# One packed weight input for a decoder trunk: every weight slab is stored as 8 KB rows, and the conv state arrives by channel

## The chip, the cores and the metric

The kernel runs on 1 core of one Trainium2 chip. The metric is the device time of one execution in microseconds. Before the change it is 1344.36 us (median of 3 runs, 1343.42 to 1346.48). The profiled execution of the same kernel took 1343.75 us, of which 1342.0 us lie between its first and last instruction (the span).

## What is computed

One layer of a decoder trunk, for 512 prompt tokens and 32 sample tokens (8 sequences of 4) with d_model 1024. All arithmetic is fp32; each big product is made of three fp32r products (a high part and a low part of each operand).

```
def layer(x, c, conv_prev, attend, w):
    mod = silu(c) @ w['w_ada'] + w['b_ada']             # 6 x 1024 columns: shifts, scales, gates
    h = rmsnorm(x, norm1) * (1 + sc1) + sh1
    bg, cg, xin, q, kc, vc, ks, vs, kw, vw, nsa_g, merge_g = split_columns(h @ w['w_in'])
    v, conv_new = short_conv(cg * xin, conv_prev, w['w_conv'], w['b_conv'])   # width 3, per channel
    y_a = (bg * v) @ w['w_out_conv']
    o_b = attend(q, gates, kv_cmp, kv_sel, kv_win)      # compressed, selected and window branches
    y_b = o_b @ w['w_o_nsa']
    x = x + g1 * ((ga * y_a + gb * y_b) @ w['w_out'])
    h2 = rmsnorm(x, norm2) * (1 + sc2) + sh2
    x = x + g2 * ((silu(h2 @ w['w_gate']) * (h2 @ w['w_up'])) @ w['w_down'])
```

The compressed branch multiplies blocks of cached K/V rows by `w_phi1` (2 x 2048 x 128). `conv_prev` is `state_conv`, the last 2 conv inputs of each of the 8 sample sequences: 16 rows of 1024 channels.

## The kernel before, in words

Activations lie transposed in SBUF: 128 channels on the partitions, 8 chunks of channels (KC), 544 tokens along the free side, worked in two halves of 288 and 256 tokens. A weight is read as a *slab* of 8 row blocks x 256 columns, 1 MB (`slab`, lines 164 to 168), into one of three `raw` buffers, by one DMA of the SP queue whose rows are 256 columns = 1 KB (512 B for `w_phi1` and for part of `w_down`). `split` (lines 170 to 178) makes a high part `wh` on ACT (line 176) and a low part `wl` on DVE (line 177) of 128 columns; each has two buffers. `mm3` (lines 180 to 183) issues the three matmuls on PE. Eight chunks x three matmuls x two halves make one linear of 48 matmuls.

Stages in order: loading and transposing x, and the compression of the cached rows with the first 8 `w_ada` slabs between (lines 357 to 574); the K, V and q projections (580 to 709); the short conv, interleaved with the attention of the sample sequences (712 to 967); the conv's output projection (983); the prompt attention with the other `w_ada` slabs and the gate `gb` between (1001 to 1180); the output projections, and the FFN.

Two loaders have loops of their own. `phi_load` (395) reads half of `w_phi1`, 16 row blocks of 128 columns. The q slabs (683 to 689) take two DMAs each, and the `w_o_nsa` slabs (1199 to 1206) four.

GpSimd (POOL) gathers the paged cache rows by indirect DMA: `gt`, 128 rows of 8 KB, 16 times (line 428, two buffers, copied by DVE at 438 and transposed by PE at 446 into `xt`), and `sraw`, 128 rows of 16 KB, 8 times (line 789, transposed by PE at 850 into `kt`).

At the start of the conv stage the SP queue loads the table `tb` (719) and the conv state `st`, 16 partitions of 4 KB (727 to 728). PE transposes `st` in 8 small transposes into the PSUM tile `stp` (732), and DVE copies it to `stT` (733), 128 channels x 8 x 16. Only a POOL copy per conv chunk reads `stT` (745). After the transposes in program order come a generator `fill` (943 to 951), whose steps are half linears of the conv (`cg`, `xin`, `bg` for each chunk), and `sample_gen` (793), which starts with the small products `sx` of q and the keys (805, 807), takes softmaxes of them with `tb` on DVE and ACT (811 to 819, result `px`), lets three more steps of `fill` run, and multiplies `px` on PE (822). `lin`, `stp`, `imp` and `kt` share one PSUM tag of five buffers.

The order of the instructions on each engine is not the program's. A planner orders them by the program's order, by which inputs its own cost model holds ready, and by free buffers. Each engine and each DMA queue then works its own list strictly in order. So the loads of `new_win_sample` (1326), which stand in the FFN's code, are issued from 25 us on.

Of the kernel before, what the change touches and what calls it, by code (L numbers as in the profile page):

```python
# [9 lines left out]
F32 = mybir.dt.float32  # L10
# [8 lines left out]
D = 1024  # L19
KC = 8  # L20
# [13 lines left out]
FC = FF // 128  # L34
# [5 lines left out]
C_KV = 4096  # L40
C_GATE = 5632
# [58 lines left out]
def build(tc, a, o):  # L100
# [19 lines left out]
    def tp_ps(nm):  # L120
        return ps.tile([128, 512], F32, tag="g", bufs=5, name=nm)
# [37 lines left out]
    def raw_tile(n):  # L159
        return wpool.tile([128, 2048], F32, tag="raw", bufs=3, name=nm(n))  # L160

    last_slab = [None]

    def slab(src, c0, nk=8, ncol=256, k0=0):
        t = raw_tile("raw")
        v = t[:, 0:nk * ncol].rearrange("p (k f) -> p k f", k=nk)
        last_slab[0] = sync.dma_start(v, src[k0 * 128:(k0 + nk) * 128, c0:c0 + ncol].rearrange("(k p) f -> p k f", p=128))
        return v

    def split(view, nk=8, perm=None):  # L170
        wh = wpool.tile([128, 8, 128], F32R, tag="wh", bufs=2, name=nm("wh"))
# [46 lines left out]

    cT = cst.tile([128, 8, 32], F32, name="cT")
    pool.memset(cT, 0.0)  # L220
    w_ada, b_off = a["w_ada"], 0

    def mod_slab(s):
        v = slab(w_ada, s * 256)
        p = tp_ps(nm("modp"))
        for k in range(KC):
            for hh in range(2):
                j = (k % 2) * 2 + hh
                pe.matmul(p[32 * j:32 * j + 32, 0:128], lhsT=cT[:, k, :], rhs=v[:, k, hh * 128:(hh + 1) * 128], start=(k < 2), stop=(k >= 6))  # L229
# [163 lines left out]
    rws = []  # L393

    def phi_load(v):
        rw = raw_tile("rphi").rearrange("p (k f) -> p k f", k=16)
        sync.dma_start(rw, a["w_phi1"][v].rearrange("(k p) f -> p k f", p=128))
        rws.append(rw)

    def phi_split(v, qt):  # L400
        qv = lambda t: t.rearrange("p (s c) f -> p s c f", s=2)[:, :, 2 * qt:2 * qt + 2, :]
# [178 lines left out]
    def kv_type(ty, rp, x32=None):  # L580
        sps = acc_ps(nm("sps"))
        for v in range(2):
            sl = slab(a["w_in"], C_KV + ty * 512 + v * 256)
            stage = rp.tile([128, 4, 256], F32, tag="stage", bufs=2, name=nm("stage"))
            for gp in range(2):
                dst = rp.tile([128, NT], F32, tag="kvT", bufs=2, name=nm("kvT"))
                linear(split(sl[:, :, gp * 128:(gp + 1) * 128]), h, lambda hf, p: act.activation(dst[:, hcols(hf)], p, AF.Copy))
                while kvp:
                    kvp.pop(0)()
                kvp.append(lambda v=v, gp=gp, dst=dst, stage=stage: kv_post(ty, v, gp, dst, stage, sps, rp, x32))  # L590
# [79 lines left out]
        cmp_prompt(v, x32, rp)  # L670
    kv_type(2, rp)

    sl = slab(a["w_in"], C_GATE, ncol=128)
    linear(split(sl), h, lambda hf, p: act.activation(gT[0:48, hcols(hf)], p[0:48, :], AF.Sigmoid))
    while kvp:
        kvp.pop(0)()
# [5 lines left out]
    pool.memset(qbd, 0.0)  # L682
    for gp in range(2):
        for rp_ in range(2):
            t = raw_tile("rq")
            tv = t.rearrange("p (k g f) -> p k g f", k=8, g=2)
            for gg in range(2):
                c0 = C_Q + (2 * gp + gg) * 256 + rp_ * 128
                sync.dma_start(tv[:, :, gg, :], a["w_in"][:, c0:c0 + 128].rearrange("(k p) f -> p k f", p=128))
            for r2 in range(2):  # L690
                r = rp_ * 2 + r2
                ch = gp * 4 + r
                w = split(tv[:, :, :, r2 * 64:(r2 + 1) * 64], perm=lambda z: z.rearrange("p k (g f) -> p k g f", g=2))
# [12 lines left out]
                for n in range(2):  # L706
                    sync.dma_start(q_dr[gp][n][:, r * TP:(r + 1) * TP], hl[n].bitcast(F32))
# [16 lines left out]
        off += w_  # L724
    t_sel, t_win, t_cmp, t_new, t_idx, t_rs, t_gs, t_gb = tbs

    st = cv.tile([16, D], F32, name="st")
    sync.dma_start(st, a["state_conv"])
    stT = cv.tile([128, 8, 16], F32, name="stT")
    p = tp_ps("stp")  # L730
    for k in range(KC):
        pe.transpose(p[:, k * 16:(k + 1) * 16], st[:, k * 128:(k + 1) * 128], ident[0:16, 0:16])
    dve.tensor_copy(stT, p[:, 0:128].rearrange("p (k n) -> p k n", k=8))
    ncv = cv.tile([128, 8, 18], F32, name="ncv")

    conv_w = {}
# [33 lines left out]

    def slab_for(nme, k):
        if k % 2 == 0:
            conv_w[nme] = slab(a["w_in"], {"cg": C_CG, "xin": C_XIN, "bg": C_BG}[nme] + k * 128)
        return conv_w[nme]

    csv = a["cache_sel"].rearrange("n t w -> (n t w)").rearrange("(x y) -> x y", y=8 * 512)
# [156 lines left out]

    def ga_linear(k):
        if k % 2 == 0:
            gsl[k // 2] = slab(a["w_in"], C_MERGE + k * 128)
        ga = gas[k] = gap_.tile([128, NT], F32, tag="ga", bufs=3, name=nm("ga"))
        w = split(gsl[k // 2][:, :, (k % 2) * 128:(k % 2) * 128 + 128])
        if k < GAF:
            return linear_gen(w, h, lambda hf, p: evac(ga[:, hcols(hf)], p))  # L940
        linear(w, h, lambda hf, p: act.activation(ga[:, hcols(hf)], p, AF.Sigmoid))
# [39 lines left out]
    C = yinf  # L981

    def y_a(k2):
        sy = slab(a["w_out_conv"], k2 * 256)
        for kk in range(2):
            k = k2 * 2 + kk
            cs = slice(kk * 128, kk * 128 + 128)
            if k >= GAF:
                ga_linear(k)
            else:  # L990
                act.activation(gas[k], gas[k], AF.Sigmoid)
            ga = gas[k]
            linear(split(sy[:, :, cs]), (yh, yl), lambda hf, p: dve.tensor_mul(C[:, k, hcols(hf)], p, ga[:, hcols(hf)]))
# [41 lines left out]
        pool.tensor_copy(vm[rs, :, r, :], vcp[rs].rearrange("p (g d) -> p g d", g=4))  # L1035
    def gb_gen():
        for k2 in range(4):
            sg = slab(a["w_in"], C_MERGE + 1024 + k2 * 256)
            for kk in range(2):
                k = k2 * 2 + kk  # L1040
                wh, wl = split(sg[:, :, kk * 128:(kk + 1) * 128])
# [155 lines left out]
    for k in range(KC):  # L1197
        to_hilo(oT[:, k, :], oh[:, k, TS:NT], ol[:, k, TS:NT])
    for k2 in range(4):
        t = raw_tile("wo")  # L1200
        for gp in range(2):
            for gg in range(2):
                pr = slice(gg * 64, gg * 64 + 64)
                r0 = (2 * gp + gg) * 256
                sync.dma_start(t[pr, gp * 1024:(gp + 1) * 1024].rearrange("p (r f) -> p r f", r=4), a["w_o_nsa"][r0:r0 + 256, k2 * 256:(k2 + 1) * 256].rearrange("(r d) f -> d r f", d=64))
        sy = t.rearrange("p (k f) -> p k f", k=8)
        for kk in range(2):
            k = k2 * 2 + kk
            cs = slice(kk * 128, kk * 128 + 128)
# [42 lines left out]
        yield  # L1252

    for k2 in range(4):
        so = slab(a["w_out"], k2 * 256)
        for kk in range(2):
            v = so[:, :, kk * 128:(kk + 1) * 128]
            if k2 == 0:
# [72 lines left out]
    for c in range(FCA, FC):  # L1331
        ffn_tiles(f6b, c)
    for c2 in range(1, FC // 2):
        sg, su = slab(a["w_gate"], c2 * 256), slab(a["w_up"], c2 * 256)
        if c2 <= DEC_B:
            win_shift(c2 - 1)
        for cc in range(2):
# [46 lines left out]
    posts = []  # L1384
    for m in range(KC):
        if m % 2 == 0:
            sc_ = slab(a["w_down"], m * 128, nk=6, ncol=256, k0=16)
        ra = slab(a["w_down"], m * 128, nk=16, ncol=128, k0=0)
        vs = [(ra[:, 0:8, :], 0, 8), (ra[:, 8:16, :], 8, 8), (sc_[:, :, (m % 2) * 128:(m % 2) * 128 + 128], 16, 6)]
        pls = [lin_ps(nm("dn"))[:, 0:HW[q]] for q in range(2)]  # L1390

# [19 lines left out]
_SHAPES = {  # L1411
    "x_prompt": (512, 1024), "x_sample": (32, 1024), "c_prompt": (1, 1024), "c_sample": (8, 1024),
    "cache_cmp": (80, 128, 512), "cache_sel": (80, 128, 512), "cache_win": (8, 512, 512),
    "state_conv": (16, 1024), "page_table": (8, 8), "w_ada": (1024, 6144), "b_ada": (6144,), "norm1": (1024,),
    "w_in": (1024, 7728), "w_conv": (3, 1024), "b_conv": (1024,), "w_out_conv": (1024, 1024),
    "pe_cmp": (2, 32, 64), "w_phi1": (2, 2048, 128), "w_phi2": (2, 128, 64), "w_o_nsa": (1024, 1024),
    "w_out": (1024, 1024), "norm2": (1024,), "w_gate": (1024, 2816), "w_up": (1024, 2816),
    "w_down": (2816, 1024), "norm_f": (1024,),
}
_OUTS = [  # L1420
    ("y_prompt", (512, 1024), (1, 512, 1024)), ("y_sample", (32, 1024), (8, 4, 1024)),
# [25 lines left out]
```

## Time and profile before

| | |
|---|---|
| median of 3 runs | 1344.36 us |
| profiled execution | 1343.75 us |
| its span, first to last instruction | 1342.0 us |
| PE busy | 1310.5 us, 98% of the span |
| DVE, ACT, POOL busy | 49%, 40%, 5% |
| SP's DMA queue | 149.98 MB in 133302 packets |
| POOL's DMA queue (gathers, window loads) | 41.95 MB in 4608 packets |

PE, DVE, ACT and POOL are TensorE, VectorE, ScalarE and GpSimd; SP issues most DMAs. In timelines a row gives the start in us, the duration, the engine, the line, the instruction, what it writes and reads, its shape and how many were merged; a bracket gives the idle time of that engine before it and what ended it. A duration of a matmul covers its pipeline, so neighbours overlap; the distance of two starts is what one costs.

### The profile page before, as it was taken

The page shows a single profiled execution, that of the slowest core. Times are in us where ns is not written, and L with a number is a line of the kernel's source. Part 1 is how long each engine was busy: PE and PEld are TensorE (multiplying, and loading weights), DVE is VectorE, ACT ScalarE, POOL GpSimd, SP SyncE. Part 2 cuts the span into 40 slices and gives each one's busy share as a digit, 9 for nine tenths or more (in the row PEclk, how much of TensorE's full clock was granted, in tenths as well). Part 3 has the DMA queues.
Part 4 walks back from the last instruction along what each step waited for, and adds up shares of the span by engine and source line. Part 5 has one row for each costly group of instructions (what it writes and reads, how often), then busy time and mean ns, then how long its engine had stood idle before and what let it go on. Part 6 is the DMA issues. An engine that isn't in the chain of part 4 may idle for free.

```text
span 1342.0 us, 25662 instructions
## 1 busy us (share of the span) xinstructions
PE 1310.5 (98%) x10840; PEld 1210.6 (90%) x10840; DVE 654.3 (49%) x1570; ACT 537.5 (40%) x1065; POOL 70.3 (5%) x123
## 2 busy tenths in 40 slices
PE   7999999997999999999999999999999999999997
PEld 6788899996999999899777777999999999999996
DVE  5559332343454454426687676667433333333335
ACT  6335233432332334324776776435323223222223
POOL 2101030001011110001000000000000000000000
PEclk8999999998999999999999999999999999999999
DMA  9996036872535562754457336532223223133221
GB/s 330 313 331 231 33 112 188 275 218 83 215 130 196 185 213 95 195 132 131 124 152 199 101 110 176 155 126 64 64 64 95 95 65 124 56 87 87 87 64 67
DMA packets 138025, 193.56 MB, mean 144 GB/s; under 512 B 4818, under 2 KB 124762, under 8 KB 132919
## 3 DMA queue, kind: packets, MB, share of 16 engines
q1 hardware_dynamic: 133302, 149.98, 36.5%
q0 software_dynamic: 4608, 41.95, 8.3%
q8 instruction: 85, 1.39, 0.5%
q14 instruction: 30, 0.24, 0.1%
HBM read 174.47 MB, written 25.76 MB: 149 GB/s over the span
## 4 chain that ended last, share of the span: by engine, by line
PE 95%; DMA 2%; DVE 1%; ACT 1%; issue 0%; SPq 0%; ACTq 0%; DVEq 0%
PE lin L181 19%; PE lin L182 19%; PE lin L183 19%; PE dn L181 3%; PE dn L182 3%; PE dn L183 3%; PE acc L1133 3%; PE ptp L1139 3%; PE phi L462 2%; PE phi L460 2%; PE phi L461 2%; PE xt L446 2%; PE modp L229 2%; PE kt L850 2%; PE sp L1108 1%; PE sp L1109 1%
## 5 line engine op out<-in xcount | busy, mean ns | idle before, releaser
L181 PE MATMUL lin<-h_hi,wh 128*128 128x288 f32 (+1 forms) x1648 | 479.4, 291 | 0.0
L182 PE MATMUL lin<-h_lo,wh 128*128 128x288 f32 (+1 forms) x1648 | 475.2, 289 | 0.0
L183 PE MATMUL lin<-h_hi,wl 128*128 128x288 f32 (+1 forms) x1648 | 473.8, 288 | 0.0
L181 PEld LDWEIGHTS lin<-h_hi,wh 128*128 128x128 f32 x1648 | 311.1, 189 | 9.4 <-issue 8.1
L182 PEld LDWEIGHTS lin<-h_lo,wh 128*128 128x128 f32 x1648 | 310.7, 189 | 0.5
L183 PEld LDWEIGHTS lin<-h_hi,wl 128*128 128x128 f32 x1648 | 310.1, 188 | 0.3
L177 DVE TENSOR_TENSOR wl<-raw,wh 128x1024 fp32r<-128x1024 f32 x132 | 159.9, 1212 | 244.5 <-ACT wh L176 244.2
L176 ACT ACTIVATE wh<-raw 128x1024 fp32r<-128x1024 f32 x132 | 137.9, 1045 | 300.0 <-PE lin L182 211.4
L181 PE MATMUL dn<-f_hi,wh 128*128 128x256 f32 (+1 forms) x352 | 101.9, 290 | 0.0
L182 PE MATMUL dn<-f_lo,wh 128*128 128x256 f32 (+1 forms) x352 | 101.3, 288 | 0.0
L183 PE MATMUL dn<-f_hi,wl 128*128 128x256 f32 (+1 forms) x352 | 101.0, 287 | 0.0
L1115 ACT ACTIVATE P<-P,nms 128x512 f32<-128x512 f32 (+3 forms) x128 | 70.6, 555 | 18.8 <-DVE nms L1114 17.9
L1114 DVE CUSTOM_DVE_ANT_0 P<-sp,ta 128x512 f32<-128x512 f32 (+3 forms) x128 | 57.5, 482 | 31.0 <-PE sp L1102 23.5
L183 PEld LDWEIGHTS dn<-f_hi,wl 128*128 128x128 f32 x352 | 66.3, 188 | 0.0
L181 PEld LDWEIGHTS dn<-f_hi,wh 128*128 128x128 f32 x352 | 66.2, 188 | 0.0
L182 PEld LDWEIGHTS dn<-f_lo,wh 128*128 128x128 f32 x352 | 66.2, 188 | 0.0
L460 PE MATMUL phi<-xh,wph 128*128 128x512 f32 x128 | 54.0, 422 | 0.0
L461 PE MATMUL phi<-xh,wpl 128*128 128x512 f32 x128 | 52.1, 407 | 0.0
L462 PE MATMUL phi<-xl,wph 128*128 128x512 f32 x128 | 52.0, 408 | 0.0
L448 ACT ACTIVATE xh<-xt 128x512 fp32r<-128x512 f32 x64 | 34.8, 597 | 32.3 <-PE xt L446 31.4
L449 DVE TENSOR_TENSOR xl<-xt,xh 128x512 fp32r<-128x512 f32 x64 | 41.0, 684 | 13.1 <-ACT xh L448 13.1
L1139 PEld LDWEIGHTS ptp<-ident,P 128*128 128x128 f32 x320 | 35.7, 141 | 10.9 <-issue 8.9
(370 smaller groups left out, 2110.2 us busy)
## 6 DMA issues: line engine op xcount, KB each, us to landing
raw<-in_w_in SPq DMA_DIRECT2D x26, 1024.0 KB, 6.6
raw<-in_w_ada SPq DMA_DIRECT2D x24, 1024.0 KB, 9.3
raw<-in_w_gate SPq DMA_DIRECT2D x11, 1024.0 KB, 5.4
raw<-in_w_up SPq DMA_DIRECT2D x11, 1024.0 KB, 5.4
wraw<-in_cache_win POOLq DMA_DIRECT2D x8, 1024.0 KB, 7.0
raw<-in_w_down SPq DMA_DIRECT2D x8, 1024.0 KB, 5.7
out_new_win_sample<-in_cache_win SPq DMA_DIRECT2D x8, 1016.0 KB, 10.5
rq<-in_w_in SPq DMA_DIRECT2D x8, 512.0 KB, 12.0
```

What stands on the lines that cost most here:

```text
L176: act.activation(oh, view, AF.Copy)
L177: dve.tensor_sub(ol, view, oh.bitcast(F32))
L181: pe.matmul(p, lhsT=wh[:, k, :], rhs=xh, start=start, stop=False)
L182: pe.matmul(p, lhsT=wh[:, k, :], rhs=xl, start=False, stop=False)
L183: pe.matmul(p, lhsT=wl[:, k, :], rhs=xh, start=False, stop=stop)
L449: dve.tensor_sub(xlb[v][:, lp * 512:lp * 512 + 512], p, xo.bitcast(F32))
L460: pe.matmul(po, lhsT=w_h, rhs=mh, start=first, stop=False)
L461: pe.matmul(po, lhsT=w_l, rhs=mh, start=False, stop=False)
L462: pe.matmul(po, lhsT=w_h, rhs=ml, start=False, stop=last)
L1114: dve.tensor_tensor_reduce(out=t[:, 0:n], in0=sps[br], in1=t_dist[:, 512 - n:512], scale=-hs, scalar=3e38, op0=ALU.add, op1=ALU.min, accum ...
L1115: act.activation(t[:, 0:n], t[:, 0:n], AF.Exp, scale=-1.0, bias=nms[:, c:c + 1], accum_out=sums[:, c:c + 1])
L1139: pe.transpose(tp[:, r * 128:(r + 1) * 128], P[br, r][:, 128 * j:128 * j + 128], ident)
```

## The change

The weights come as one input `wt` of 128-partition slabs, laid out before the launch. Each slab is one DMA of 128 contiguous rows, 8 KB for a full slab (6 KB for the tails of `w_down`, 4 KB for the gate slab). The two DMAs of a q slab, and the four of a `w_o_nsa` slab, become one each. `phi_load` goes through `slab`. The conv state comes as 128 channels x 128 numbers and is loaded straight into `stT`; the tile `st`, the eight transposes and the copy are gone. Nothing else in the program's order is changed.

```
+def _slabs():
+    r = np.arange(1024).reshape(8, 128)
+    ...
+    for v in range(2):
+        d["phi", v] = ("w_phi1", np.arange(2048).reshape(16, 128) + 2048 * v, np.arange(128))
+    for s in range(24):
+        add(("ada", s), "w_ada", r, s * 256, 256)
+    ...
-    def slab(src, c0, nk=8, ncol=256, k0=0):
-        t = raw_tile("raw")
-        v = t[:, 0:nk * ncol].rearrange("p (k f) -> p k f", k=nk)
-        last_slab[0] = sync.dma_start(v, src[k0 * 128:(k0 + nk) * 128, c0:c0 + ncol].rearrange("(k p) f -> p k f", p=128))
-        return v
+    def slab(*key):
+        nk, ncol = len(SLABS[key][1]), len(SLABS[key][2])
+        v = raw_tile("raw")[:, 0:nk * ncol]
+        last_slab[0] = sync.dma_start(v, a["wt"][SLAB_AT[key], :, 0:nk * ncol])
+        return v.rearrange("p (k f) -> p k f", k=nk)
...
     def phi_load(v):
-        rw = raw_tile("rphi").rearrange("p (k f) -> p k f", k=16)
-        sync.dma_start(rw, a["w_phi1"][v].rearrange("(k p) f -> p k f", p=128))
-        rws.append(rw)
+        rws.append(slab("phi", v))
...
-            t = raw_tile("rq")
-            tv = t.rearrange("p (k g f) -> p k g f", k=8, g=2)
-            for gg in range(2):
-                c0 = C_Q + (2 * gp + gg) * 256 + rp_ * 128
-                sync.dma_start(tv[:, :, gg, :], a["w_in"][:, c0:c0 + 128].rearrange("(k p) f -> p k f", p=128))
+            tv = slab("q", gp, rp_).rearrange("p k (g f) -> p k g f", g=2)
...
-    st = cv.tile([16, D], F32, name="st")
-    sync.dma_start(st, a["state_conv"])
     stT = cv.tile([128, 8, 16], F32, name="stT")
-    p = tp_ps("stp")
-    for k in range(KC):
-        pe.transpose(p[:, k * 16:(k + 1) * 16], st[:, k * 128:(k + 1) * 128], ident[0:16, 0:16])
-    dve.tensor_copy(stT, p[:, 0:128].rearrange("p (k n) -> p k n", k=8))
+    sync.dma_start(stT.rearrange("p k n -> p (k n)"), a["state_conv"])
...
-        t = raw_tile("wo")
-        for gp in range(2):
-            for gg in range(2):
-                ...
-                sync.dma_start(t[pr, gp * 1024:(gp + 1) * 1024]...)
-        sy = t.rearrange("p (k f) -> p k f", k=8)
+        sy = slab("o", k2)
...
+    st = np.asarray(inputs["state_conv"]).reshape(16, 8, 128)
+    arrs["state_conv"] = np.ascontiguousarray(st.transpose(2, 1, 0)).reshape(128, 128)
```

The other calls of `slab` name their slab by a key in place of a source and a column, and load the same numbers into the same places.

## Rows read from the trace of the kernel before

**Rows 1.** The page: the busy time of the engines, and the shares of the chain that ended last.

```profile
PE 1310.5 (98%) x10840; PEld 1210.6 (90%) x10840; DVE 654.3 (49%) x1570; ACT 537.5 (40%) x1065; POOL 70.3 (5%) x123
PE 95%; DMA 2%; DVE 1%; ACT 1%; issue 0%; SPq 0%; ACTq 0%; DVEq 0%
```

**Rows 2.** The waits of PE over the whole run, the longest first: the tile it stood before, what ended the wait, us in total, times, the longest.

```profile
PE stp L732 <- DMA st<-in_state_conv: 8.7, 1, 8.7
PE xtp L507 <- DMA xr<-in_x_prompt: 5.7, 1, 5.7
PE xt L446 <- DVE gt L438: 1.8, 1, 1.8
PE yt L1365 <- DVE x L1360: 1.5, 1, 1.5
...
PE kt L850 <- DMA sraw<-in_cache_sel,ixs: 0.5, 1, 0.5
```

**Rows 3.** The timeline of PE around the transposes of the conv state.

```profile
304.71 0.32 PE L805 MATMUL sx<-kcs,qbd 128*32 128x63 f32 x8
304.84 0.29 PE L807 MATMUL sx<-kn,qbd 128*32 128x64 f32 x8
313.83 1.03 PE L732 MATMUL stp<-ident,st 16*128 16x16 f32 x8 [8.70 <-DMA st<-in_state_conv]
314.80 0.61 PE L181 MATMUL lin<-h_hi,wh 128*128 128x288 f32 x1
...
318.08 0.37 PE L182 MATMUL lin<-h_lo,wh 128*128 128x288 f32 x1
318.30 0.29 PE L183 MATMUL lin<-h_hi,wl 128*128 128x288 f32 x1
318.43 0.29 PE L181 MATMUL lin<-h_hi,wh 128*128 128x288 f32 x1
...
327.03 0.33 PE L822 MATMUL imp<-px,tb 128*128 128x64 f32 x2
```

**Rows 4.** Stretches of the start and of this place: us, busy time (and instructions) of PE, PEld, DVE, ACT and POOL, the granted clock of PE as a share of 2.4 GHz, the busy share of the 16 DMA engines, GB/s.

```profile
14.70:16.50 1.80, 0.01 (x1) 0.02 (x1) 0.83 (x2) 1.72 (x3) 0.00 (x0) 1.00 1.07 402
18.00:20.00 2.00, 2.00 (x15) 1.67 (x13) 1.84 (x4) 1.98 (x5) 0.18 (x1) 0.50 1.04 299
24.00:26.00 2.00, 2.00 (x33) 1.43 (x35) 0.53 (x1) 1.98 (x3) 0.75 (x1) 0.83 1.08 319
305.00:308.00 3.00, 0.14 (x12) 0.00 (x0) 1.71 (x2) 2.40 (x3) 0.00 (x0) 1.00 0.29 107
308.00:313.80 5.80, 0.00 (x0) 0.00 (x0) 0.36 (x4) 0.00 (x0) 0.00 (x0) 0.50 0.71 234
313.80:318.00 4.20, 4.17 (x21) 4.13 (x22) 0.98 (x10) 0.44 (x2) 0.20 (x1) 0.50 0.00 0
318.00:320.00 2.00, 2.00 (x17) 2.00 (x16) 0.00 (x0) 0.18 (x1) 0.00 (x0) 0.94 0.00 0
```

**Rows 5.** The same place on the other engines: SP's queue, then ACT, then DVE (three timelines). `wh` and `wl` at 298.72 to 301.04 and at 304.70 to 307.02 are the weights of the first `cg` and the first `xin` linear.

```profile
307.56 0.32 SPq L707 DMA_DIRECT2D q_dr1l<-ql  x1
307.98 0.37 SPq L719 DMA_DIRECT2D tb<-in_tab_b  x1
308.44 0.39 SPq L728 DMA_DIRECT2D st<-in_state_conv  x1
...
298.72 1.06 ACT L176 ACTIVATE wh<-raw 128x1024 fp32r<-128x1024 f32 x1 [2.21 <-PE lin L182]
304.70 1.06 ACT L176 ACTIVATE wh<-raw 128x1024 fp32r<-128x1024 f32 x1 [2.21 <-PE lin L182]
314.15 0.19 ACT L816 ACTIVATION_READ_ACCUMULATOR px<-sxs,n 128x1 f32 x1
319.82 0.41 ACT L741 ACTIVATE cg<-lin 128x288 f32<-128x288 f32 x1 [5.48 <-PE lin L183]
...
313.44 0.28 DVE L801 TENSOR_TENSOR gm<-tb,gT 48x128 f32<-48x128 f32 x1 [5.91 <-DMA tb<-in_tab_b]
314.90 0.29 DVE L733 COPY stT<-stp 128x128 f32<-128x128 f32 x1 [0.74 <-PE stp L732]
315.30 0.25 DVE L819 TENSOR_SCALAR px<-px,rc 128x63 f32<-128x63 f32 x1
323.67 1.23 DVE L177 TENSOR_TENSOR wl<-raw,wh 128x1024 fp32r<-128x1024 f32 x1 [8.11 <-ACT wh L176]
327.71 0.16 DVE L825 COPY G<-imp 128x3 f32<-128x3 f32 x1 [1.36 <-PE imp L823]
```

**Rows 6.** The chain that ended last, its first pieces: start, us, what.

```profile
5.47 10.18 DMA gt<-in_cache_cmp,ixc
15.67 0.70 DVE gt L438
16.51 2.69 PE xt L446 x16
```

**Rows 7.** The DMA queues between 12.3 and 13.6 us: packets, MB, the time of the packets as a share of 16 DMA engines. q0 is POOL's queue, q1 is SP's.

```profile
q0 software_dynamic: 50, 0.40, 81.5%
q1 hardware_dynamic: 49, 0.10, 20.3%
```

**Rows 8.** SP's queue between 309.5 and 313.5 us, while `tb` (128 rows of 8016 B) and `st` land.

```profile
q1 hardware_dynamic: 164, 1.00, 69.2%
```

**Rows 9.** The DMA queues between 436.5 and 441 us, while the `sraw` gather issued at 429.93 us shares the engines with a slab; then its time from issue to landing.

```profile
q0 software_dynamic: 101, 1.41, 73.6%
q1 hardware_dynamic: 150, 0.14, 15.7%
...
sraw<-in_cache_sel,ixs POOLq DMA_INDIRECT x1, 12.2
```

**Rows 10.** DVE's waits for `gt` landings between 15 and 160 us (total, times, longest), and two of the copies.

```profile
DVE gt L438 <- DMA gt<-in_cache_cmp,ixc: 5.2, 4, 1.7
...
55.63 0.69 DVE L438 COPY gt<-gt 128x1024 f32<-128x1024 f32 x1 [1.67 <-DMA gt<-in_cache_cmp,ixc]
```

**Rows 11.** The page's row of POOL's queue over the whole span; then SP's queue between 930 and 1160 us, where it moves almost nothing but slabs with 1 KB rows.

```profile
q0 software_dynamic: 4608, 41.95, 8.3%
...
q1 hardware_dynamic: 19729, 19.89, 27.4%
```

More of the change, by code (lines that the diff above doesn't have):

```diff
@@ L92, in _tables, with add @@
     return ts, ta, tb
+def _slabs():
+    r = np.arange(1024).reshape(8, 128)
+    d = {}
+    def add(key, src, rows, c0, n):
+        d[key] = (src, rows, np.arange(c0, c0 + n))
+    for v in range(2):
+        d["phi", v] = ("w_phi1", np.arange(2048).reshape(16, 128) + 2048 * v, np.arange(128))
+    for s in range(24):
+        add(("ada", s), "w_ada", r, s * 256, 256)
+    for ty in range(3):
+        for v in range(2):
+            add(("kv", ty, v), "w_in", r, C_KV + ty * 512 + v * 256, 256)
+    add(("gate",), "w_in", r, C_GATE, 128)
+    for gp in range(2):
+        for rp in range(2):
+            c = np.concatenate([np.arange(128) + C_Q + (2 * gp + gg) * 256 + rp * 128 for gg in range(2)])
+            d["q", gp, rp] = ("w_in", r, c)
+    for k2 in range(4):
+        for n, c in (("cg", C_CG), ("xin", C_XIN), ("bg", C_BG), ("ga", C_MERGE), ("gb", C_MERGE + 1024)):
+            add((n, k2), "w_in", r, c + k2 * 256, 256)
+        add(("oc", k2), "w_out_conv", r, k2 * 256, 256)
+        p = np.arange(128)
+        j = np.arange(8)
+        rows = (2 * (j[:, None] // 4) + p[None, :] // 64) * 256 + (j[:, None] % 4) * 64 + p[None, :] % 64
+        add(("o", k2), "w_o_nsa", rows, k2 * 256, 256)
+        add(("out", k2), "w_out", r, k2 * 256, 256)
+        add(("dc", k2), "w_down", np.arange(2048, 2816).reshape(6, 128), k2 * 256, 256)
+    for c2 in range(FC // 2):
+        add(("fg", c2), "w_gate", r, c2 * 256, 256)
+        add(("fu", c2), "w_up", r, c2 * 256, 256)
+    for m in range(8):
+        add(("da", m), "w_down", np.arange(2048).reshape(16, 128), m * 128, 128)
+    return d
+SLABS = _slabs()
+SLAB_AT = {k: i for i, k in enumerate(SLABS)}
 TS_W = 3 + 16 + 8 + 8 + 16 + 1
@@ L220, in build @@
     pool.memset(cT, 0.0)
-    w_ada, b_off = a["w_ada"], 0
     def mod_slab(s):
-        v = slab(w_ada, s * 256)
+        v = slab("ada", s)
         p = tp_ps(nm("modp"))
@@ L582, in kv_type @@
         for v in range(2):
-            sl = slab(a["w_in"], C_KV + ty * 512 + v * 256)
+            sl = slab("kv", ty, v)
             stage = rp.tile([128, 4, 256], F32, tag="stage", bufs=2, name=nm("stage"))
@@ L671, in build @@
     kv_type(2, rp)
-    sl = slab(a["w_in"], C_GATE, ncol=128)
+    sl = slab("gate")
     linear(split(sl), h, lambda hf, p: act.activation(gT[0:48, hcols(hf)], p[0:48, :], AF.Sigmoid))
@@ L772, in slab_for @@
         if k % 2 == 0:
-            conv_w[nme] = slab(a["w_in"], {"cg": C_CG, "xin": C_XIN, "bg": C_BG}[nme] + k * 128)
+            conv_w[nme] = slab(nme, k // 2)
         return conv_w[nme]
@@ L935, in ga_linear @@
         if k % 2 == 0:
-            gsl[k // 2] = slab(a["w_in"], C_MERGE + k * 128)
+            gsl[k // 2] = slab("ga", k // 2)
         ga = gas[k] = gap_.tile([128, NT], F32, tag="ga", bufs=3, name=nm("ga"))
@@ L983, in y_a @@
     def y_a(k2):
-        sy = slab(a["w_out_conv"], k2 * 256)
+        sy = slab("oc", k2)
         for kk in range(2):
@@ L1037, in gb_gen @@
         for k2 in range(4):
-            sg = slab(a["w_in"], C_MERGE + 1024 + k2 * 256)
+            sg = slab("gb", k2)
             for kk in range(2):
@@ L1199, in build @@
     for k2 in range(4):
-        t = raw_tile("wo")
-        for gp in range(2):
-            for gg in range(2):
-                pr = slice(gg * 64, gg * 64 + 64)
-                r0 = (2 * gp + gg) * 256
-                sync.dma_start(t[pr, gp * 1024:(gp + 1) * 1024].rearrange("p (r f) -> p r f", r=4), a["w_o_nsa"][r0:r0 + 256, k2 * 256:(k2 + 1) * 256].rearrange("(r d) f -> d r f", d=64))
-        sy = t.rearrange("p (k f) -> p k f", k=8)
+        sy = slab("o", k2)
         for kk in range(2):
@@ L1254, in build @@
     for k2 in range(4):
-        so = slab(a["w_out"], k2 * 256)
+        so = slab("out", k2)
         for kk in range(2):
@@ L1299, in ffg @@
         return f6.tile([128, NT], F32, tag="ffg", bufs=2, name=nm("ffg"))
-    sg, su = slab(a["w_gate"], 0), slab(a["w_up"], 0)
+    sg, su = slab("fg", 0), slab("fu", 0)
     p6.close()
@@ L1333, in build @@
     for c2 in range(1, FC // 2):
-        sg, su = slab(a["w_gate"], c2 * 256), slab(a["w_up"], c2 * 256)
+        sg, su = slab("fg", c2), slab("fu", c2)
         if c2 <= DEC_B:
@@ L1386, in build @@
         if m % 2 == 0:
-            sc_ = slab(a["w_down"], m * 128, nk=6, ncol=256, k0=16)
-        ra = slab(a["w_down"], m * 128, nk=16, ncol=128, k0=0)
+            sc_ = slab("dc", m // 2)
+        ra = slab("da", m)
         vs = [(ra[:, 0:8, :], 0, 8), (ra[:, 8:16, :], 8, 8), (sc_[:, :, (m % 2) * 128:(m % 2) * 128 + 128], 16, 6)]
@@ L1413 @@
     "cache_cmp": (80, 128, 512), "cache_sel": (80, 128, 512), "cache_win": (8, 512, 512),
[L1414 to L1418, printed above, removed]
+    "page_table": (8, 8), "b_ada": (6144,), "norm1": (1024,),
+    "w_conv": (3, 1024), "b_conv": (1024,),
+    "pe_cmp": (2, 32, 64), "w_phi2": (2, 128, 64),
+    "norm2": (1024,), "norm_f": (1024,),
+}
+_WEIGHTS = {
+    "w_ada": (1024, 6144), "w_in": (1024, 7728), "w_out_conv": (1024, 1024), "w_phi1": (4096, 128),
+    "w_o_nsa": (1024, 1024), "w_out": (1024, 1024), "w_gate": (1024, 2816), "w_up": (1024, 2816), "w_down": (2816, 1024),
 }
@@ L1430, in _arrays @@
     arrs = {k: np.ascontiguousarray(np.asarray(inputs[k])).reshape(s) for k, s in _SHAPES.items()}
+    w = {k: np.asarray(inputs[k]).reshape(s) for k, s in _WEIGHTS.items()}
+    wt = np.zeros((len(SLABS), 128, 2048), np.float32)
+    for i, (src, rows, cols) in enumerate(SLABS.values()):
+        t = w[src][rows.T[:, :, None], cols[None, None, :]]
+        wt[i, :, 0:rows.shape[0] * len(cols)] = t.reshape(128, -1)
+    arrs["wt"] = wt
+    st = np.asarray(inputs["state_conv"]).reshape(16, 8, 128)
+    arrs["state_conv"] = np.ascontiguousarray(st.transpose(2, 1, 0)).reshape(128, 128)
     arrs["tab_s"], arrs["tab_a"], arrs["tab_b"] = _tables()
```

## The prediction

> **What bounds it now.** I read the page first: PE is busy 98% of the span and carries 95% of the chain that ended last [rows 1]. So a change can only pay by taking work or idle time off PE. Next the waits of PE [rows 2]. The reader is to see two things: no row names a `raw` slab, so no weight load is ever late for PE; and the longest wait, 8.7 us, stands before the transposes of the conv state, which the change deletes. Then the timelines around that wait on PE [rows 3] and the others [rows 5], the granted clock [rows 4], and, because the change makes all slab rows long, who shares the DMA engines with the slabs where a gather is waited for [rows 6 to 9].
>
> **Term 1, the wait for the conv state.** PE ends `sx` at 305.13 (313.83 less 8.70 idle), stands until `st` has landed, and spends 313.83 to 314.80 on the eight transposes [rows 3]. Both go: 8.70 + 0.97 = 9.7 us. The wait also costs clock. PE has 1.00 (2.4 GHz) until 308 and 0.50 (1.2 GHz) from then until some 318 [rows 4]. From 314.80 to 318.08 there are 13 matmul intervals, 0.25 us each, against some 0.13 us from 318.30 on [rows 3]: 13 x 0.12 = 1.5 us more. Together −11.2 us.
>
> What is late next? PE's list goes on with the `cg` linear, whose `wh` and `wl` were ready at 301, and the `xin` linear, ready at 307 [rows 5]. These run from 314.80 until the product on `px` at 327.03 [rows 3]: 12.2 us, at full clock 10.7. Started at 305.13 they last to 315.8. `px` needs `tb`, which lands at 313.4; it was ready at 315.55, and there DVE had stood for the `stT` copy at 314.90 [rows 5]. With that copy gone the reciprocal can follow ACT's last piece at 314.34, so `px` is there at about 314.8. One us to spare: `tb` takes the place of `st`, but behind 10.7 us of PE work. The five PSUM buffers are just enough: two halves of `cg`, two of `xin`, one `imp`.
>
> ACT works in order, so the `cg` copies (first at 319.82) now queue behind the exponential that waits for `tb`, and with them the split of `bg`, then DVE's `wl` (323.67) and `G` (327.71) [rows 5]. ACT is free at 314.34; two copies of 0.4, a split of 1.06, then 1.23 of `wl` and 0.6 of conv products put `G` at about 317.6, where a plain shift by 11.2 puts it at 316.5. PE meanwhile has the `kt` transposes and the `xin` rest. I take **+0.5**, with 0 (all hidden) and +1.5 as ends.
>
> The new load into `stT` is the same 64 KB at the same place in SP's list. Its reader is now POOL's copy, with the other POOL work of the conv and DVE's `xin` products queued behind it. `st` landed at 313.8 [rows 3]; that product is due when the first `xin` half ends, at 305.1 + 6.0 + 3.2 = 314.3. Half a us of cover: 0. If the load came later, PE would feel it only through `xin`'s PSUM.
>
> **Term 2, slabs as long rows.** As a transfer time this is worth nothing: PE never waits for a slab, and three buffers cover it. The DMAs saved (4 for q, 12 for `w_o_nsa`) are SP's, and SP is not what PE waits for; the cover is again the slab buffers. But packets are not hidden where a gather is. Between 12.3 and 13.6 us POOL's queue had 50 packets, 0.40 MB, and SP's 49, 0.10 MB [rows 7]: turn by turn, 8 KB against 2 KB. So the gather held four fifths of the engines. Its packet costs 0.815 x 1.3 x 16 / 50 = 0.34 us of one engine, the `w_phi1` packet 0.203 x 1.3 x 16 / 49 = 0.086. The first `gt`, 128 packets, is 8 per engine: 8 x (0.34 + 0.086) = 3.4 us. SP's packets are as long as its rows: `tb` and `st` came in 164 packets for 1.00 MB, over 6 KB each [rows 8]. After the change `w_phi1` has 8 KB rows, and the gather's share becomes a half: 8 x 0.68 = 5.4 us. **+2.0 us** on that landing, and it heads the chain: gather, copy, transposes at 16.51 [rows 6]; PE already idles 1.8 us for it [rows 2, 4]. SP's 2 MB of `w_phi1` last long enough, 16 such packets per engine.
>
> The Trainium skill (DMA: Bandwidth & Descriptors, Queues, rings and completion order) has this rule: a DMA engine takes turns between queues packet by packet, whatever the length. The equal counts agree with it; were bytes shared evenly instead, this term would be 0.
>
> PE at the start also has the low clock, 0.50 from 18 to about 24.5 [rows 4], after an idle stretch that now becomes 3.8 us. **+0.5** if it lasts longer with it (ends −0.5 and +1.5, the whole of the other stall's clock loss).
>
> The same in the conv stage: the `sraw` gather of 429.93 takes 12.2 us and PE stands 0.5 us for it [rows 2, 9]. Its window shows 101 packets against 150, 1.41 MB against 0.14 [rows 9]; SP's packets used 0.157 x 4.5 = 0.7 us per engine. With 8 KB packets up to 8 x 0.31 = 2.5 us go between. That is 1.8 more if the whole slab falls into the gather, less what the slab before it ends earlier: **+1.5**, ends 0 and +2.5.
>
> The fifteen other `gt` gathers: DVE waits for four, 5.2 us in all, the longest 1.7 [rows 10], and PE for none but the first [rows 2], since a copy runs ahead of its transposes. **+0.5** for what DVE's list holds up behind them; ends 0 and +4 (2.0 on two of them).
>
> **Sum.** −11.2 + 0.5 + 2.0 + 0.5 + 1.5 + 0.5 = −6.2. Against the profiled execution, 1343.75, that is 1337.6; the median is 0.6 above that execution, so **1338.0**.
>
> **Rivals.**
>
> *A: the gathers are not delayed.* Long packets also cost less engine time per MB: POOL's queue took 8.3% of 1342 us for 41.95 MB, 2.66 us per MB; slabs with 1 KB rows took 27.4% of 230 us for 19.89, 3.17 us per MB [rows 11]. So `w_phi1` could be out of the way sooner, and the 1.8 us idle before `xt` go as well. −11.2 + 0.5 − 1.8 gives 1331.9. Against it: the equal counts. Chance 0.20. The Trainium skill (DMA: Bandwidth & Descriptors, Specifications) says that transfers reach line rate from 512 B up; the trace disagrees by those 16%, and by that rule this rival would lose its ground.
>
> *B, the side that is slower: `tb` takes the whole place of `st`.* The planner puts the product on `px` right behind `sx`, ahead of the `cg` and `xin` linears; it already put `sx` ahead of them. Then PE stands from 305.13 to 314.8, 9.7 us at the same low clock, only the transposes are saved, and term 2 stays: −8.7 − 1.0 + 9.7 + 4.5 = +4.5, or 1348.9. If term 2 stays away as well, 1344.4. It decides as soon as `px` stands before 10 us of PE work. Against it: in program order three steps of `fill` lie between. Chance 0.08.
>
> *C: every gather pays.* Term 2 hits the gathers of the first 130 us one by one: 7 x 2.0 = 14 us more, 1352. It decides where a gather is later than its copy's lead on the transposes. Against it: PE waits for none of them now, DVE at most 1.7 us. Chance 0.06; half of that comes to no more than 1346.
>
> **Numbers.** The forecast has 0.66; all its lower ends together give 1334.7, all its upper ends 1344.7. Under 0.2% (2.7 us) a measurement of this kernel can tell nothing from no change: faster means under 1341.7, slower over 1347.0. Faster: 0.61 of the forecast and all of A, 0.81. Slower: 0.05 of B and 0.03 of C, 0.08. The rest, 0.11, is the same. The range goes from A's 1331.9 less 0.9 to 1343.0, where the forecast's upper ends have met but for the last 1.7 us; it leaves out most of B and C and some 0.03 of the forecast.
>
> **What would show it.** Right: no row `stp`; PE goes from `sx` into `lin` without a gap, at clock 1.00 through 305 to 320; DVE still waits for `tb` until about 313; the first `gt` takes about 12 us and PE's wait before `xt` is 3 to 4 us; SP's queue has about as many packets as POOL's rows do, 8 KB each, and PE's wait for `sraw` is about 2 us. Wrong: a new wait of PE of several us before `imp` (B); a first `gt` landing before 15.7 us (A); PE waiting for `xt` several times (C); or an order on PE so different that the rows of before answer to nothing.

## The result, and the profile after

The changed kernel takes 1332.54 us (median of 4 runs, 1331.51 to 1333.26) against 1343.89 for the kernel before on the same chip: a ratio of 0.9911, interval 0.9894 to 0.9929. That is 11.35 us less, where the forecast had 6. The direction was right and the time lies in the range, but the gain is nearly twice what was forecast. The profiled execution took 1332.59 us with a span of 1330.8.

The page of the kernel after, its engines, its chain and its two DMA queues [rows 1, 11 answer to them]:

```profile
PE 1306.2 (98%) x10832; PEld 1206.7 (91%) x10832; DVE 652.3 (49%) x1569; ACT 537.9 (40%) x1065; POOL 69.7 (5%) x123
PE 95%; DMA 2%; DVE 1%; ACT 0%; issue 0%; POOL 0%; POOLq 0%; ACTq 0%; DVEq 0%
...
q1 hardware_dynamic: 30630, 149.98, 33.4%
q0 software_dynamic: 4608, 41.95, 8.3%
```

The kernel is bound as it was, by PE. SP moves the same 149.98 MB in 30630 packets instead of 133302. PE's waits, as in [rows 2]:

```profile
PE xtp L545 <- DMA xr<-in_x_prompt: 5.6, 1, 5.6
PE xt L484 <- DVE gt L476: 2.7, 1, 2.7
...
PE imp L851 <- POOL ncv L787: 0.7, 1, 0.7
```

The row `stp` is gone and no new row of several us stands in its place. The wait before `xt` grew from 1.8 to 2.7, but not because the gather landed later. The chain's first pieces [rows 6 before]:

```profile
5.42 10.13 DMA gt<-in_cache_cmp,ixc
15.57 0.70 DVE gt L476
16.41 2.92 PE xt L484 x16
```

The gather took 10.13 us (10.18 before) and `xt` starts at 16.41 instead of 16.51. PE merely ended the transposes ahead of it sooner (13.71 us, before 14.71).

Where did the 11 us go? The view of one tile gives the first and the last start of its matmuls, so it shows how far the two runs have drifted apart at that point. After:

```profile
L484 PE MATMUL xt<-ident,gt x256: 270/273/421, 16.4 to 153.2; 128*128 128x128 f32 x128
L898 PE MATMUL ss<-kt,qbd x96: 592/605/617, 321.9 to 521.7; 128*32 128x512 f32 x96
L1137 PE MATMUL sp<-kh,qs x64: 334/393/504, 611.5 to 779.8; 128*128 128x512 f32 x32, 128*128 128x384 f32 x32
L280 PE MATMUL modq<-ident,m x24: 272/328/329, 41.5 to 813.2; 128*128 128x128 f32 x24
```

Before, the same tiles start at 16.5 and end at 153.5 (`xt`), start at 332.5 (`ss`), at 622.4 (`sp`), and the last `modq` is at 824.4. So the drift is −0.1 at the first `xt`, −0.3 at its last, −10.6 at the first `ss`, −10.9 at `sp` and −11.2 at the end. Of it, 10.3 us fall between 153 and 332: that is term 1's place, and nearly nothing came from anywhere else, for better or worse.

PE's timeline there [rows 3 before], then stretches of it (columns as in [rows 4], the granted clock behind POOL's busy time), then DVE:

```profile
310.44 0.32 PE L834 MATMUL sx<-kcs,qbd 128*32 128x63 f32 x8
...
317.77 0.41 PE L851 MATMUL imp<-px,tb 128*128 128x64 f32 x2 [0.72 <-POOL ncv L787]
```

```profile
304.00:308.00 4.00, 4.00 (x33) 4.00 (x32) 1.71 (x2) 1.68 (x3) 0.00 (x0) 1.00 0.19 69
308.00:314.00 6.00, 6.00 (x62) 5.77 (x61) 1.23 (x1) 2.77 (x4) 0.00 (x0) 1.00 0.75 228
314.00:318.00 4.00, 3.28 (x28) 3.10 (x27) 1.92 (x13) 1.41 (x4) 0.52 (x3) 1.00 0.00 0
```

```profile
314.73 0.29 DVE L830 TENSOR_TENSOR gm<-tb,gT 48x128 f32<-48x128 f32 x1
...
317.09 0.42 DVE L781 TENSOR_TENSOR up<-lin,cg 128x256 f32<-128x256 f32 x1 [1.26 <-PE lin L224]
317.43 0.24 DVE L848 TENSOR_SCALAR px<-px,rc 128x63 f32<-128x63 f32 x1
```

PE is busy without a gap from 304 to 314 at clock 1.00, where it had stood at 0.50 before. The planner's order is another than I assumed: the whole `cg` linear now runs ahead of `sx` (310.44, where it was 304.71), since no transpose waits behind `sx` any more. `px` is made at 317.43, behind the product of the second `xin` half in DVE's list, and PE stands 0.72 us for it. DVE never waits for `tb` now: it reaches `gm` at 314.73, after the first `xin` half. The page names POOL's `ncv`, but `imp` reads `px`, which ended at 317.67, just before `imp` started.

### The profile page after: what moved, and what is told of

Same layout as the page of the kernel before. It is cut to its first block, busy times and chain, and to the rows that moved or that the text cites. A ratio compares the mean times of both kernels' runs of the same rounds, so it can differ in the third digit from the quotient of the medians.

```text
span 1330.8 us, 25612 instructions
## 1 busy us (share of the span) xinstructions
PE 1306.2 (98%) x10832; PEld 1206.7 (91%) x10832; DVE 652.3 (49%) x1569; ACT 537.9 (40%) x1065; POOL 69.7 (5%) x123
## 3 DMA queue, kind: packets, MB, share of 16 engines
q1 hardware_dynamic: 30630, 149.98, 33.4%
## 4 chain that ended last, share of the span: by engine, by line
PE 95%; DMA 2%; DVE 1%; ACT 0%; issue 0%; POOL 0%; POOLq 0%; ACTq 0%; DVEq 0%
PE lin L222 19%; PE lin L223 19%; PE lin L224 19%; PE dn L223 3%; PE dn L222 3%; PE dn L224 3%; PE acc L1162 3%; PE ptp L1168 3%; PE phi L500 2%; PE phi L498 2%; PE phi L499 2%; PE xt L484 2%; PE modp L269 2%; PE kt L879 2%; PE sp L1137 1%; PE sp L1138 1%
## 5 line engine op out<-in xcount | busy, mean ns | idle before, releaser
L218 DVE TENSOR_TENSOR wl<-raw,wh 128x1024 fp32r<-128x1024 f32 (+1 forms) x148 | 178.6, 1207 | 266.1 <-ACT wh L217 265.5
L217 ACT ACTIVATE wh<-raw 128x1024 fp32r<-128x1024 f32 (+1 forms) x148 | 154.9, 1046 | 329.6 <-PE lin L223 236.2
L1168 PEld LDWEIGHTS ptp<-ident,P 128*128 128x128 f32 x320 | 35.7, 141 | 10.9 <-issue 8.9
```

Of the source, the lines that this page charges most:

```text
L217: act.activation(oh, view, AF.Copy)
L218: dve.tensor_sub(ol, view, oh.bitcast(F32))
L1168: pe.transpose(tp[:, r * 128:(r + 1) * 128], P[br, r][:, 128 * j:128 * j + 128], ident)
```

## The experiments

**One part alone.** The kernel before with only the conv state laid out by channel:

```
-    st = cv.tile([16, D], F32, name="st")
-    sync.dma_start(st, a["state_conv"])
-    ... eight pe.transpose, dve.tensor_copy(stT, ...)
+    sync.dma_start(stT.rearrange("p k n -> p (k n)"), a["state_conv"])
```

> The kernel before with the new conv state alone (loaded by channel into stT, no transposes); every weight slab as before. Theory S (the whole gain is the wait for the conv state, its transposes and the clock it cost): 1332.5 to 1333.5 us, PE's wait of 8.7 us gone, a landing of the first gt near 15.6 us. Theory L (the long rows give a part of the gain, 2 to 4 us): 1335 to 1337. Theory P (the prediction's second term is real, 4 us lost to the long rows, and the conv state gives more than the 11.2 us reckoned): about 1328.

It took 1333.54 us, ratio 0.9917 (0.9904 to 0.9930). And the kernel after with the conv state as before, so that only the slabs differ:

> The changed kernel with the conv state as before (16 rows, eight transposes, a copy); all weights packed in 8 KB rows. Theory S: 1343.2 to 1344.4 us, the same as before, with the 8.7 us wait back. Theory L: 1340 to 1342. Theory P: 1347 to 1348.

It took 1343.95 us, ratio 0.9993 (0.9984 to 1.0001). The first has the whole gain, the second none. The wait at `stp` is back. The wait before `xt` is the one of the kernel before, but that does not go by the slabs: the run with the state alone, with the old slabs, has 2.6.

```profile
PE stp L766 <- DMA st<-in_state_conv: 8.9, 1, 8.9
...
PE xt L484 <- DVE gt L476: 1.8, 1, 1.8
```

So the long rows neither cost nor bring anything that can be told from nothing in the whole time (the interval runs from 2.2 us less to 0.1 us more), and term 2 of the forecast (+4.5 us) is wrong.

**The wait alone.** The kernel after with one transpose of `stT`, into a tile that nobody reads, where the eight had stood:

```
+    p = tp_ps("stp")
+    pe.transpose(p[0:16, 0:128], stT[:, 0, :], ident)
```

> The changed kernel with one PE transpose of stT put where the eight stood, its result used by nothing: one PE instruction that waits for the load, everything else as in the changed kernel. Theory S: PE stands again until the load lands at about 313.5 us: 1341 to 1343.5. If the planner puts it behind the cg linear, or the wait was not the cause: 1332.5 to 1334.

1342.63 us, ratio 0.9986 (0.9978 to 0.9995), with PE's row:

```profile
313.64 0.38 PE L764 MATMUL stp<-ident,stT 128*16 128x128 f32 x1 [8.63 <-DMA stT<-in_state_conv]
```

One instruction of 0.38 us that waits brings back 10.1 us (1342.63 − 1332.54) of the 11.35. The work of the transposes is the small rest; the wait, with the clock that it costs, is the gain. The expectation had everything else as in the kernel after, and that was not so: with the transpose the planner also gave back the order of before, `sx` at 304.6 and the transpose behind it, ahead of the `cg` linear. The two belong together. The state is no earlier in the kernel after (its load is issued at 308.17 there and at 308.28 here); but no PE instruction reads it any more, so nothing that waits for it stands ahead of `cg`.

**Why the wait was long.** The kernel before with the two loads exchanged on SP's queue, `st` first and `tb` behind it:

> The kernel before with the loads of `st` and `tb` exchanged: `st` (64 KB) first on SP's queue, `tb` (1 MB) behind it; nothing else. Theory F (the wait for `st` was in good part the 1 MB ahead of it in the queue): `st` is issued at about 308.0 and lands some 2.5 to 3.5 us later (256 KB stores took 2.2 in this stretch) instead of at 313.8; PE's wait falls from 8.7 to about 5.5 to 6.5, median 1341.0 to 1342.5. Theory I (the wait is set by the issue and the latency of a load): the wait stays over 8 us, median 1344. If PE's later wait for `px`, which needs `tb`, grows by what the wait for `st` loses, the median is 1344 also, and the trace shows it at `imp`.

1341.94 us, ratio 0.9983 (0.9975 to 0.9992). PE's wait went from 8.7 to 6.3, and the chain shows the load:

```profile
308.18 3.42 DMA st<-in_state_conv
```

3.42 us from issue to landing, where `st` behind `tb` had taken 313.8 − 308.4 = 5.4 [rows 3, 5]. Some two us of the wait were the 1 MB ahead of it in the queue, as theory F had it. The other 6.3 are the load's own 3.4 and the 2.8 by which PE was ready before it was issued (308.18, less 311.65 − 6.3 = 305.35, the end of `sx`).

**Loading the state early, a surprise.** I expected that the old layout would do as well if `st` came early enough. The kernel before with `st` loaded at the start, into free rows of `xs`, and transposed there:

```
+    sync.dma_start(xs[96:112, 0:D], a["state_conv"])
...
+            for k in range(KC):
+                pe.transpose(sp_[:, k * 16:(k + 1) * 16], st[:, k * 128:(k + 1) * 128], ident[96:112, 96:112])
```

> The kernel before with the conv state loaded at the start beside x_sample and transposed there, the work on PE kept and only its place moved; weights as before. Theory S: the wait of 8.7 us and the 1.5 us of clock go, the transposes stay at 0.8 to 1.0 us among the first ones: 1333.3 to 1335. If PE's work on the transposes or the layout of the state were what mattered, not the wait: 1342 to 1344.

A miss: 1358.36 us, ratio 1.0102 (1.0088 to 1.0117), 14 us slower than before instead of 10 faster. Its longest waits on PE, and SP's and DVE's rows at the longest:

```profile
PE imp L821 <- DVE px L818: 11.5, 1, 11.5
...
PE gtp L685 <- ACT gT L680: 4.6, 1, 4.6
```

```profile
330.83 0.38 SPq L167 DMA_DIRECT2D raw<-in_w_in  x1
331.31 0.52 SPq L725 DMA_DIRECT2D tb<-in_tab_b  x1
```

```profile
338.58 0.28 DVE L800 TENSOR_TENSOR gm<-tb,gT 48x128 f32<-48x128 f32 x1 [4.40 <-DMA tb<-in_tab_b]
```

The planner had given another order. A slab load that waited for its buffer until 330.83 stood ahead of `tb`, which had been issued at 307.98 before; `px` came 12 us after PE had done all that stood before `imp`. My reading then was that `tb`'s place in the queue was the cost. To test it, `st` came early as 128 rows of 512 bytes on SP's queue with one transpose at the old place, and `tb` on POOL's queue:

```
-    sync.dma_start(tb, a["tab_b"])
+    pool.dma_start(tb, a["tab_b"])
...
+    pe.transpose(p[:, 0:128], st, ident)
```

> The kernel before with `st` loaded at the start as 128 rows of 512 bytes into a tile of its own (0.5 KB a partition) and turned by one PE transpose instead of eight, and with `tb` loaded on POOL's queue instead of SP's. The run with early transposes was 14 us slower than before: with the state there early the planner lets the convolution's work start sooner, and a slab load that waits for its buffer got ahead of `tb` on SP's queue, so PE waited 11.5 us for `px` at 328 to 340. Theory Q (that queue place is the cost): with `tb` on POOL's queue, issued by about 275, the wait at `imp` is under 1 us and the median falls to 1343 to 1346 (1358.4 less 11.5, less some 1 to 2 us of low clock behind it and 1 us of transposes; the wait of 4.6 us at the gate's transposes and that of 1 us at 303 stay). Theory R (the loss comes from the early transposes or from another shared resource): still 1354 to 1359.

1354.15 us, ratio 1.0075 (1.0060 to 1.0090): a miss for that theory. `tb` was issued at 274.82 and no longer late, yet the wait stayed:

```profile
PE imp L821 <- DVE px L818: 7.4, 1, 7.4
```

```profile
329.24 1.23 DVE L177 TENSOR_TENSOR wl<-raw,wh 128x1024 fp32r<-128x1024 f32 x1 [5.31 <-ACT wh L176]
...
333.25 0.80 DVE L756 SCALAR_TENSOR_TENSOR v<-up,vec,v 128x560 f32<-128x560 f32 x1
333.97 0.28 DVE L800 TENSOR_TENSOR gm<-tb,gT 48x128 f32<-48x128 f32 x1
```

So `tb`'s queue place was worth about 4.1 us of the 11.5; the two kernels differ in the transposes too, but DVE's own wait for `tb` in the run before this one, 4.40, says the same. What is left comes with the order on DVE: the chain to `px`, from `gm` on, stands behind a weight split and the conv products, which themselves wait for the linear that PE has just ended. PE has nothing left to do meanwhile.

**The same early load without another order.** What the two slow kernels share is one more load among the first of SP's queue. So `st` was loaded early on POOL's queue instead, behind the first two gathers, with the one transpose of the run before and with `tb` back on SP's queue; the order on PE, ACT and DVE is then that of the run with the new state alone, but for the one transpose and its copy:

```
+    pool.dma_start(st, a["state_conv"].rearrange("n (k p) -> (n k) p", p=128))
```

> The kernel before, weights and conv state laid out as before; `st` is loaded early (128 rows of 512 bytes, on POOL's queue, behind the first gathers) and turned by one PE transpose instead of eight, at the place of the eight. No load is added to SP's queue at the start. The planner's order on PE, ACT and DVE is that of the run with the new state alone (1333.5 us), but for the one transpose and its copy. Theory W (the change's whole gain is the wait for `st`, and the loss of the two other early-state runs was the planner's order, which an added early load on SP's queue changes): no wait at `stp` over 0.3 us, no wait at `imp` over 1.5 us, median 1333 to 1335. Theory E (loading the state early costs of itself, or the gain needs the layout by channel): over 1338.

1333.46 us, ratio 0.9921 (0.9907 to 0.9934), theory W. The transpose has no wait, and that at `imp` is 0.9:

```profile
306.61 0.27 PE L731 MATMUL stp<-ident,st 128*128 128x128 f32 x1
```

So the gain needs neither the layout by channel nor the packed weights: a state that is there in time and one PE transpose of 0.27 us do the same within what can be measured. And loading early is not what cost 14 us; that came with the other order. Which part of that order costs what is not separated: against the run with the new state alone, the kernel with early transposes is 3.9 us behind at the last `xt` (157.0 against 153.1), 8.6 at the gate's transposes (264.0 against 255.4) and 22.5 at the first `imp` (340.1 against 317.6).

**Packet length where a gather is waited for.** Two kernels, equal but for one more 1 MB load on SP's queue behind the first compression slab, so that SP's queue is never empty while the first `gt` gather moves: once in rows of 8 KB, once in pieces of 1 KB.

```
+    sync.dma_start(vext.rearrange("p b f -> p (b f)"), a["wt"][SLAB_AT["ada", 0], :, :])       # 8 KB
...
+    sync.dma_start(vext, a["wt"][s0:s0 + 8, :, 0:256].rearrange("s p f -> p s f"))              # 1 KB
```

> The kernel after with one more load of 1 MB on SP's queue, behind the first compression slab and ahead of the first gather's issue, so that SP's queue always has packets while the first `gt` gather moves; its packets are rows of 8 KB. Theory T (turns go packet by packet, whatever their length, as the forecast had it): the gather's 8-KB packets each wait for one 8-KB packet; the first `gt` lands 1.5 to 3 us later than in the kernel after (issue at 5.4, landing at 15.55 there), at 17 to 18.5, and 1 to 2 us later than with short rows. Theory N (what the gather loses to the other queue doesn't hang on the length of its rows): within 0.4 us of the run with short rows.

> As the run with long rows, and the same bytes, but in pieces of 1 KB. Theory T: the first `gt` gather gives up only 1 KB a turn and lands at 15.5 to 16.3, 1 to 2 us before the run with long rows; the extra load itself takes longer. Theory N: it lands within 0.4 us of the run with long rows.

With long rows the gather took 10.9 us from its issue (5.38) to its landing, with short ones 9.96 (5.89 to 15.85), one profiled execution of each. The issues differ by 0.5 us, so I compare the durations: about 0.95 us for the length, between theory N's 0.4 and theory T's 1 to 2. Among the kernels without the added load that keep the order of before or of after, the same duration differs by no more than 0.2 us (10.05 to 10.27). Against the 10.13 of the kernel after it is +0.8 and −0.2, where T had +1.5 to +3 and 0 to +0.7. The DMA queues between 14 and 15 us show the turns. Long rows, then short rows:

```profile
q1 hardware_dynamic: 32, 0.22, 53.2%
q0 software_dynamic: 28, 0.20, 47.1%
```

```profile
q0 software_dynamic: 46, 0.34, 83.3%
q1 hardware_dynamic: 48, 0.05, 13.3%
```

Nearly equal counts in both, 47% of the engines for the gather against 83%. The turns are as the forecast read them; what they do to this landing was not. The whole times (1352.45 and 1354.42, one run each) tell nothing of packets: the added load on SP's queue brought the other order again, with PE waits of 11.0 us at `imp` and 3.6 at the gate's transposes in both.

## Why the prediction was half right

**Term 1 was right**, in mechanism and size: forecast −11.2 and +0.5 = −10.7, measured −10.3 between 153 and 332. The wait and the eight transposes are gone (8.70 + 0.97), the clock stays at 1.00 where it was 0.50 (1.5 of the forecast). The cost entered as +0.5 for queues behind `tb` came as 0.72 at `imp`, on another path: not ACT's `cg` copies (307.75 and 311.40 now, ahead of the exponential at 315.20), but DVE's list, with `px` behind an `xin` product. The spare of one us for `px` was close, and on the wrong side by 0.7. The planner's moving of `cg` ahead of `sx` was not foreseen: behind `sx` only the `xin` linear was left to cover `px`, some 6 us and not the 10.7 reckoned, and that this cost no more than 0.72 was in part luck.

**Term 2 is the step that failed.** The forecast priced four delays of gathers by long packets: +2.0 for the first `gt`, +0.5 for a longer low clock behind it, +1.5 for `sraw`, +0.5 for the rest. Measured by the drift they are −0.1 at the first `xt`, −0.2 more by the last, and −0.3 from 332 to 622, with `sraw` in it; the run with the slabs alone is the kernel before (0.9993). Without them the sum is −10.7, or 1333.0 against the profiled 1343.75; it took 1332.59. That is near rival A's outcome, which had 0.20, though not by all of its reasons: the 1.8 us before `xt`, which A had gone, became 2.7. The +2.0 was the one price without a lower end, and 1332.54 lies under all lower ends of the forecast together (1334.7); the time is in the range only because the range reached to A. (The sum as written gives 1337.6 + 0.6 = 1338.2, not 1338.0; nothing hangs on it.)

Why did the first gather not pay? The turns were there: 39 packets against 42 between 12 and 13 us before, 28 against 22 after. The Trainium skill (DMA: Bandwidth & Descriptors, Queues, rings and completion order) says that an engine changes queues packet by packet; the trace agrees. Kernel before, 10 to 11 us and then 12 to 13 us (`w_phi1` came in packets of 2 KB, though its rows are 512 B):

```profile
q1 hardware_dynamic: 123, 0.25, 89.5%
q0 software_dynamic: 7, 0.06, 15.9%
...
q0 software_dynamic: 39, 0.32, 84.1%
q1 hardware_dynamic: 42, 0.09, 22.7%
```

Kernel after, 10 to 11, 12 to 13, 13 to 14, and 14 to 14.5 us:

```profile
q1 hardware_dynamic: 34, 0.28, 67.2%
q0 software_dynamic: 15, 0.12, 29.3%
...
q0 software_dynamic: 28, 0.23, 54.9%
q1 hardware_dynamic: 22, 0.18, 43.4%
...
q0 software_dynamic: 37, 0.30, 72.9%
q1 hardware_dynamic: 36, 0.12, 29.8%
...
q0 software_dynamic: 26, 0.20, 101.6%
q1 hardware_dynamic: 23, 0.01, 6.8%
```

Between 12 and 13 us the share fell from 84% to 55%, as forecast. But the forecast took the one window from 12.3 to 13.6 [rows 7] for the whole transfer, and two other stretches differ. At its beginning the gather's packets come slowly: before, 7 between 10 and 11 us beside 123 of SP's, which is not turn by turn; after, 15 beside 34. And from 13 us on SP's queue gave short packets in the kernel after too (36 for 0.12 MB, then 23 for 0.01): the small load `perow`, 32 rows of 512 B, stands there between the two `w_phi1` slabs (its issue at 5.52, theirs at 5.03 and 6.93). By 14 us POOL's queue had moved 0.95 MB before and 0.84 after, 13 packets of 8 KB less; in the next half us, beside `perow`, it had the engines to itself, and the landings are equal (15.65 and 15.55). So the 2 MB of `w_phi1` that the forecast counted on did not stand beside the gather to its end; with SP's queue kept full of long rows 0.8 us showed.

What was forecast for the first gather came to the second. It is issued at about 6.9 us, and between 15 and 17 us SP's queue gave hardly anything but 8 KB rows in the kernel after. POOL's queue in these two us, then the issue with its time to landing, before and after:

```profile
q0 software_dynamic: 78, 0.62, 82.2%
...
gt<-in_cache_cmp,ixc POOLq DMA_INDIRECT x1, 12.1
...
q0 software_dynamic: 57, 0.45, 54.0%
...
gt<-in_cache_cmp,ixc POOLq DMA_INDIRECT x1, 13.9
```

That is 1.7 us more (12.15 and 13.88), and 1.9 in the run with the slabs alone: the forecast's price, nearly to the size. But it lands at 20.8, and DVE copies it at 21.85, behind other work; nobody waits for it. The mechanism was right, then, and what failed was to put it on a transfer that is waited for. The +0.5 for the clock fell with the +2.0: the granted clock between 24 and 26 us was 0.91 after, 0.83 before [rows 4].

`sraw` failed for another reason: the slab is all but through when the gather begins. The gather's first packet comes between 4 and 5 us after its issue, the slab is issued 1.0 us after it. Before, from the gather's issue to 436 us, SP's queue had moved 0.91 MB of the slab, and the rest went turn by turn with the gather [rows 9]. After, in the same 6.1 us from the issue (419.3 to 425.4), it had moved all of it, and hardly anything stood beside the gather in the time that answers to [rows 9] (425.9 to 430.4):

```profile
q1 hardware_dynamic: 893, 0.91, 49.9%
...
q1 hardware_dynamic: 143, 1.05, 52.5%
...
q0 software_dynamic: 102, 1.43, 74.1%
q1 hardware_dynamic: 11, 0.08, 11.4%
```

Slabs in long rows are shorter on the engines, as rival A had it: SP's queue took 0.365 x 1342.0 / 149.98 = 3.27 us per MB before and 0.334 x 1330.8 / 149.98 = 2.96 after. The landing took 11.9 us instead of 12.2, and PE's wait fell from 0.5 to 0.2. The median time to landing of all sixteen `gt` gathers fell from 7.8 to 6.8 us.

The Trainium skill (DMA: Bandwidth & Descriptors, Specifications) has line rate from 512 B up; the trace disagrees by those 10%. They are worth nothing here, since PE waits for no slab in either kernel.

**The rivals.** B (`tb` takes the place of `st`) did not come in the kernel after, 0.7 instead of 9.7 us. A wait of its size is real, though: in the order that four of the other kernels got, PE stood 7.4 to 11.5 us at just this `imp`. Its condition was put rightly (`px` before too little PE work: there only some 6 us of it, the `xin` linear, lay between `sx` and `imp`); but `tb` behind `st` was not the cause: in three of the four `tb` was issued late, and in the fourth, where it had been there long before, DVE's list made the wait. Its chance of 0.08 was luck as much as reading, since the order decides it and the trace of before does not show the order to come. C did not come: no wait of PE for a second `xt`, although the second gather was late.

## What to carry to other kernels

An 8.7 us wait that heads the list of the binding engine's waits is worth its length plus the clock behind it, if what is late next has cover; that part could be read from the trace to within half a us. A price worked out from one window of a transfer is not the price of its landing: look at its first and last us, at what else stands in the other queue, and at who waits for it, before it is multiplied over other transfers. And where a planner orders the work, an edit as small as one load more can cost more than the stall it cures (14 us here against 10): compare the order before the time.

## What was not expected of the chip

- A gather's packets start slowly: issued at 5.47 us, 8 of its 128 had moved by 11 us, while the other queue moved 123 short ones in the last of these us alone. Why is not shown.
- A 64 KB load behind no more than a 256 KB store took 3.42 us from issue to landing; behind 1 MB it took 5.4.
- Equal turns between the two queues, 28 against 32 packets and 46 against 48, at packet lengths that differ by a factor of eight.
- The length of the rows shows in SP's own time too: the issue that follows the first half of `w_phi1` took 4.05 us before, behind rows of 512 B, and that behind the second 7.55; after, behind rows of 8 KB, 0.35 and 0.40. PE waits for none of these loads in either kernel.
